# Norm factors spread over the partitions by a row in DRAM, and a new TensorE order for the first stage, in a hybrid decoder layer

## The chip, the core and the metric

The kernel runs on one core of a Trainium2 chip. Its time is the device time of one execution in microseconds (us); lower is better. The core has five engines that run side by side: TensorE (PE in the profile: matrix products into PSUM; PEld is its weight loading), VectorE (DVE), ScalarE (ACT), GpSimd (POOL) and SyncE (SP), which here issues nearly all DMAs. Each engine works its own list of instructions strictly in order, and an instruction that waits holds up everything behind it on its engine. That holds for SP's list of DMAs too.

## The reference

2048 prompt tokens and 8 decode tokens (2056 columns in the kernel) pass one layer of width 1024:

```python
xn = rmsnorm(x, norm1_g)
xr, gr, q, k, v = split(xn @ w_in)                  # 512 | 512 | 512 | 128 | 128
rec = rglru(causal_conv(xr)) * gelu(gr)             # gated recurrence over the tokens
att = sink_attention(q, k, v)                       # window of 128 earlier tokens, 8 heads on 2 kv heads
h = x + concat(rmsnorm(rec), rmsnorm(att)) @ w_out
hn = rmsnorm(h, norm2_g)
y = h + (silu(hn @ w_gate) * (hn @ w_up)) @ w_down  # 2816 wide
out = rmsnorm(y, final_norm_g)
# rmsnorm(x, g) = x * rsqrt(mean(x*x) + 1e-6) * g
```

There are five norms (x, rec, att, h, y). Each gives one factor per token. Activations lie with the features on the 128 partitions and the tokens along the free dimension, so a factor has to be present on all partitions as a row over the tokens before DVE can multiply with it.

## The kernel before

**Tiling.** The first part takes the tokens in four pieces (SUBS: 520 columns, then three of 512). For piece s the names end in s: input projection (ip, 14 column blocks of w_in, each by three products of high and low parts), conv, gates (g) and scan, attention items (s, pt, o), the norms of the two groups (rc for the recurrence, at for attention), output projection (op) and the norm of h. The second part is the FFN in three token groups (gi 0, 1, 2), each in two halves of 342 or 344 columns (HALVES), over 11 pairs of column blocks of w_gate, w_up and w_down. A pair is computed by seven products of sums of blocks (Strassen's scheme) for gate (ps_g), up (ps_u) and down (pd or pw); the sums of weight blocks are made by ACT, DVE and POOL out of loaded pieces (ru, rg, rd) or loaded ready-made (w_u from split_u, w_g from split_g). DVE adds the products up in SBUF: c_g, c_u for gate and up, y for down. A PSUM tile such as ps_g 1 is taken by two of the seven products in turn, so the second can start only when DVE has added up the first. finish applies the last norm to a group that is done while TensorE is already in the next group (gi 0 and 1); finish_last does it for gi 2 at the end.

**A norm factor before the change.** The sums of squares (acc) go through TensorE against a column of constants (st_...), which leaves a factor's argument per token in columns: cols[p, j] belongs to token j*w + p of the piece (w is 104, 128, 86 or 114; j up to 5). DVE adds epsilon, POOL raises to the power -1/2. row_bcast then makes the row: for each j one fp32 product of the column, repeated along the free dimension as stationary operand, with the identity, into a PSUM tile (bc_...), which ACT copies to SBUF (rb_...). Products are padded by filler products (w_...) where a table asks for it. half_bcast does the same for the norm of h out of the tile rs2, once for each half (hb).

**What sets the order.** Steps are generators (yield t) that run by planned time; the time becomes a priority, and a scheduler places the instructions of every engine by it, with one exception: TensorE's list from the start to the second pair of group 0 is written out by hand in the table PE_ORDER (name of a step, a colon, number of its products). All engines but TensorE, and TensorE behind the table, follow the scheduler. Buffers rotate: rb tiles have 3, hb tiles 2, ready-made weights (wp, wp2) 5 and 3, the PSUM tile of st, bc, hb and g has 1. A DMA on SP waits also until the eighth before it has landed.

Of the kernel before, what the change touches and what calls it, by code (L numbers as in the profile page):

```python
# [112 lines left out]
w_st_x0:13 ip0_1_0 ip0_1_1 w_st_x0:4 ip0_12_0 ip0_12_1 ip0_1_0:2 ip0_1_1:2 ip0_12_0:2 ip0_12_1:2 ip0_1_0 ip0_1_1  # L113
ip0_12_0 ip0_12_1 ip0_1_0:2 ip0_1_1:2 ip0_12_0:2 ip0_12_1:2 ip0_1_0 ip0_1_1 ip0_12_0 ip0_12_1 ip0_1_0:2 ip0_1_1:2
ip0_12_0 ip0_1_0 ip0_1_1 ip0_12_0:2 ip0_12_1:3 ip0_1_0:2 ip0_1_1 ip0_1_0 ip0_1_1:2 ip0_12_0:3 ip0_12_1:3 ip0_1_0:3
ip0_1_1:3 ip0_12_0 ip0_1_0:2 ip0_1_1:2 ip0_12_0 ip0_1_0 ip0_1_1 ip0_12_0:4 ip0_12_1:6 ip0_1_0:3 ip0_1_1:3 ip0_12_0:3
ip0_1_0:2 ip0_1_1:2 ip0_12_0:2 ip0_12_1:5 ip0_9_0:5 st_x0:5 ip0_9_0:9 ip0_9_1:24 ip0_9_0:10 bc_x0_0:4 ip0_8_0:24
ip0_8_1:4 bc_x0_4 ip0_8_1:20 ip0_0_0:24 ip0_0_1:23 g0_1_0_0 ip0_0_1 ip0_3_0:24 g0_1_0_260 ip0_3_1:17 g0_1_1_0
ip0_3_1:7 ip0_11_0:18 g0_1_1_260 ip0_11_0:6 ip0_11_1:15 vt0_0 ip0_11_1:9 ip0_10_0:23 vt0_1 ip0_10_0 ip0_10_1:24
ip0_13_0:10 vt0_2 ip0_13_0:14 ip0_13_1:6 vt0_3 ip0_13_1:18 ip0_2_0:7 s0_0_0:4 ip0_2_0:5 g0_0_0_0 s0_0_1:4 ip0_2_0:12  # L120
ip0_2_1:6 s0_1_0:4 s0_1_1:4 ip0_2_1:2 g0_0_0_260 ip0_2_1:13 pt0_0_1:4 ip0_2_1 s1_0_0:4 ip0_2_1:2 ip0_5_0:3 s1_0_1:4
ip0_5_0 g0_0_1_0 ip0_5_0:9 o0_0_0 ip0_5_0:11 ip0_5_1 s1_1_0:4 ip0_5_1:2 pt0_1_1:4 o0_0_0 ip0_5_1:4 g0_0_1_260
ip0_5_1:12 s1_1_1:2 o0_1_0 s1_1_1:2 ip0_5_1:5 ip0_4_0:6 s2_0_0:4 ip0_4_0:3 o0_1_0 ip0_4_0:11 pt1_0_0:4 ip0_4_0:2
s2_0_1:4 ip0_4_0:2 ip0_4_1:24 ip1_8_0:15 ip0_6_0:2 o1_0_0 ip0_6_0:8 pt1_0_1 o1_0_0 pt1_0_1:3 ip0_6_0 ip1_8_0
g0_3_0_0 ip0_6_0:13 ip0_6_1 ip1_8_0:2 ip0_6_1:15 o1_0_1 g0_3_0_260 s2_1_0:4 ip0_6_1 ip1_8_0 ip0_6_1 pt1_1_0
ip0_6_1:5 o1_0_1 s2_1_1:4 pt1_1_0:3 ip0_6_1 ip1_8_0:5 ip1_9_0 g0_3_1_0 ip1_9_0:19 ip0_7_0:9 ip1_9_0:2 pt1_1_1 o1_1_0
pt1_1_1:3 g0_3_1_260 ip1_9_0:2 ip0_7_0:2 o1_1_0 ip0_7_0:13 w_bc_x1_0 bc_x1_0 s3_0_0:3 s3_0_1:4 ip0_7_1 s3_0_0
ip0_7_1 o1_1_1:2 bc_x1_0 w_pt2_0_0:4 ip0_7_1 bc_x1_0 ip0_7_1 bc_x1_0 ip0_7_1:2 pt2_0_0:4 ip0_7_1:18 ip1_10_0:2
o2_0_0:2 pt2_0_1:3 g0_2_0_0 ip1_10_0:12 pt2_0_1 ip1_10_0:10 ip1_11_0:2 o2_0_1 ip1_11_0 s3_1_0:4 pt2_1_0:4 g0_2_0_260
ip1_11_0 s3_1_1:4 ip1_11_0:2 o2_0_1 ip1_11_0:11 g0_2_1_0 pt2_1_1:3 ip1_11_0:7 ip1_4_0:4 o2_1_0 ip1_4_0 pt2_1_1  # L130
ip1_4_0 o2_1_0 g0_2_1_260 ip1_4_0:18 ip1_0_0:2 o2_1_1 ip1_0_0 vt1_0 ip1_0_0:6 dS:2 o2_1_1 pt3_0_0:4 ip1_0_0:5 dS:6
ip1_0_0:6 o3_0_0 ip1_0_0:4 ip1_12_0:2 dS2:2 ip1_12_0:2 pt3_0_1 o3_0_0 ip1_12_0:2 pt3_0_1:3 ip1_12_0:18 ip1_13_0:6
o3_0_1 ip1_13_0:2 o3_0_1 ip1_13_0:3 pt3_1_0:4 ip1_13_0:9 dS3 ip1_13_0 dS3 ip1_13_0:3 ip1_1_0:8 pt3_1_1:2 o3_1_0
pt3_1_1 ip1_1_0:2 pt3_1_1 o3_1_0 dS4:4 s4_0_0 ip1_1_0:2 o3_1_1 s4_0_1:3 s4_0_0:3 s4_0_1 dS4:4 ip1_1_0 o3_1_1
ip1_1_0:11 ip1_5_0:6 dS5:2 s4_1_0:2 s4_1_1:4 ip1_5_0 vt1_1 ip1_5_0:3 s4_1_0:2 ip1_5_0:8 pt4_0_0:2 ip1_5_0 pt4_0_0:2
ip1_5_0:5 ip1_2_0:2 s5_0_0:4 ip1_2_0 s5_0_1:4 ip1_2_0 vt1_2 ip1_2_0:8 o4_0_0 ip1_2_0:6 pt4_0_1 o4_0_0 pt4_0_1:3
ip1_2_0:3 vt1_3 ip1_2_0:3 o4_0_1 s5_1_0:4 s5_1_1:4 o4_0_1 st_rc0 pt4_1_0:4 st_rc0:4 ip1_6_0:15 pt4_1_1:4 bc_rc0_0:3
# [1592 lines left out]
```

## Time and profile before

| | us |
|---|---|
| median of 3 runs (2059.78, 2065.76, 2065.12) | 2065.12 |
| span of the profiled execution, first to last instruction | 2054.6 |
| TensorE busy (98% of the span) | 2015.9 |
| VectorE busy (71%) | 1459.9 |
| ScalarE busy (46%) | 944.6 |
| GpSimd busy (44%) | 906.5 |

The profiled execution's own time is its span, 2054.6, and what lies around it before the first and after the last instruction, which the profile does not show; the median of the runs is 10.5 above the span. A row of a group reads: line, engine, operation, output<-inputs with tile numbers left out, count | busy us, mean ns of one | idle time of the engine just before, with what ended it. A row of the timeline reads: start, us, engine, line, operation, count, and in brackets idle time and its releaser. A matrix product in fp32 leaves two records. On average TensorE runs at a granted clock of 0.997 of full speed.

### The profile page before, as it was taken

The numbers are of one execution on the slowest core, as the hardware profiler recorded it, in microseconds if no ns is written. First come the engines' busy times: TensorE is split into PE (matmuls) and PEld (weight loads), VectorE is DVE, ScalarE is ACT, GpSimd is POOL, SyncE is SP. The second block draws the span as 40 slices with busy tenths as digits, with TensorE's granted clock in tenths as the row PEclk, the third lists the DMA queues.
The fourth block names the chain that finished last, engine by engine and source line by source line (L and its number), as shares of the span: only waits on it lengthen the run. The fifth ranks groups of instructions, "written<-read, shape, count | busy, mean of one in ns | idle before, by whom it ended". The sixth has DMA issues, their size and how long they took to land.

```text
span 2054.6 us, 34857 instructions
## 1 busy us (share of the span) xinstructions
PE 2015.9 (98%) x12319; PEld 1908.1 (93%) x12319; DVE 1459.9 (71%) x2694; ACT 944.6 (46%) x1960; POOL 906.5 (44%) x799
## 2 busy tenths in 40 slices
PE   9999999999999999999999999999999999999998
PEld 9988787878777899999999999999999999999998
DVE  6877886767985766666654667777768666777675
ACT  6764774553664543343334533333335433433343
POOL 5311342020122787567656645556457522322333
PEclk9999999999999999999999999999999999999999
DMA  9864584576688856666546677776677675566652
GB/s 329 293 213 143 188 275 159 175 233 210 208 261 280 314 200 223 205 210 207 207 172 210 229 260 258 227 229 221 222 253 265 211 251 189 183 197 196 197 179 96
DMA packets 208991, 450.98 MB, mean 219 GB/s; under 512 B 25232, under 2 KB 82720, under 8 KB 208800
## 3 DMA queue, kind: packets, MB, share of 16 engines
q1 hardware_dynamic: 205184, 445.73, 65.2%
q10 hardware_dynamic: 3632, 3.02, 0.4%
q8 instruction: 97, 1.59, 0.3%
q14 instruction: 78, 0.64, 0.1%
HBM read 335.89 MB, written 113.84 MB: 219 GB/s over the span
## 4 chain that ended last, share of the span: by engine, by line
PE 77%; DVE 9%; DMA 6%; ACT 3%; issue 2%; POOL 1%; SPq 0%; DVEq 0%; ACTq 0%; POOLq 0%
PE ps_u L396 19%; PE ps_g L396 19%; PE pw L396 11%; PE pd L396 10%; PE ip L396 10%; PE op L396 4%; DMA n<-hs 3%; DMA xs<-in_xT 1%; DMA m<-mixed 1%; PE o L396 1%; PE pt L401 1%; DVE sc L974 1%; DVE sc L963 1%; PE s L396 1%; DMA mixed<-n 1%
## 5 line engine op out<-in xcount | busy, mean ns | idle before, releaser
L396 PE MATMUL ps_g<-hn,w_g 128*128 128x342 f32 (+1 forms) x2772 | 489.4, 320 | 4.6 <-DVE c_u L1410 1.8
L396 PE MATMUL ps_u<-hn,w_u 128*128 128x342 f32 (+1 forms) x2772 | 479.9, 319 | 1.9 <-ACT c_u L1436 1.3
L396 PEld LDWEIGHTS ps_g<-hn,w_g 128*128 128x128 f32 x2772 | 445.1, 188 | 6.0 <-DVE c_u L1410 2.3
L396 PEld LDWEIGHTS ps_u<-hn,w_u 128*128 128x128 f32 x2772 | 444.2, 188 | 2.6 <-ACT c_u L1436 1.6
L396 PE MATMUL ip<-xn,w_in 128*128 128x512 f32 (+1 forms) x1680 | 353.4, 358 | 1.9 <-ACT xn L431 1.8
L396 PEld LDWEIGHTS ip<-xn,w_in 128*128 128x128 f32 x1680 | 270.1, 189 | 46.0 <-issue 3.8
L1500 DVE TENSOR_TENSOR y<-y,pw 128x342 f32<-128x342 f32 x504 | 238.7, 504 | 73.0 <-PE pw L396 72.2
L396 PE MATMUL pd<-fh,w_d 128*128 128x344 f32 (+1 forms) x960 | 239.4, 320 | 0.6 <-DVE y L1469 0.6
L396 PE MATMUL op<-mix,w_out 128*128 128x512 f32 (+1 forms) x960 | 203.4, 357 | 0.5 <-DVE rrec L763 0.3
L396 PEld LDWEIGHTS op<-mix,w_out 128*128 128x128 f32 x960 | 155.4, 188 | 29.3 <-issue 5.0
L1469 DVE TENSOR_TENSOR y<-y,pd 128x344 f32<-128x344 f32 (+1 forms) x240 | 117.9, 507 | 75.3 <-PE pd L396 70.7
L396 PEld LDWEIGHTS pd<-fh,w_d 128*128 128x128 f32 x960 | 168.3, 188 | 1.4 <-DVE y L1469 1.1
L396 PE MATMUL pw<-fh,wd 128*128 128x342 f32 x576 | 165.6, 319 | 1.2 <-DVE y L1500 1.2
L396 PE MATMUL pd<-fl,w_d 128*128 128x344 f32 (+1 forms) x480 | 153.4, 320 | 0.0
L1381 DVE TENSOR_TENSOR fl<-c_u,fh 128x342 fp32r<-128x342 f32 (+1 forms) x132 | 107.1, 815 | 48.3 <-ACT fh L1380 47.9
L1225 POOL TENSOR_TENSOR w_u<-ru,w_u 128x512 fp32r<-128x512 f32 x44 | 58.9, 1338 | 181.6 <-ACT w_u L1224 155.0
L1392 POOL TENSOR_TENSOR c_u<-c_u,c_g 128x342 f32<-128x342 f32 (+1 forms) x60 | 60.5, 1008 | 170.7 <-DVE c_u L1410 132.1
L1380 ACT CAST fh<-c_u 128x342 fp32r<-128x342 f32 (+1 forms) x132 | 63.0, 480 | 157.8 <-POOL c_u L1392 61.9
L396 PE MATMUL pw<-t,wd 128*128 128x342 f32 x648 | 126.7, 320 | 2.6 <-DVE t L1381 1.7
L1410 DVE TENSOR_TENSOR c_u<-c_u,ps_u 128x342 f32<-128x342 f32 (+1 forms) x99 | 50.2, 507 | 100.3 <-PE ps_u L396 100.1
L396 PEld LDWEIGHTS pw<-t,wd 128*128 128x128 f32 x648 | 106.0, 188 | 4.4 <-DVE t L1381 2.5
L396 PEld LDWEIGHTS pw<-fh,wd 128*128 128x128 f32 x576 | 105.3, 189 | 1.7 <-DVE y L1500 1.5
(316 smaller groups left out, 3507.4 us busy)
## 6 DMA issues: line engine op xcount, KB each, us to landing
w_g<-split_g SPq DMA_DIRECT2D x88, 512.0 KB, 4.2
w_u<-split_u SPq DMA_DIRECT2D x88, 512.0 KB, 4.9
w_in<-split_w SPq DMA_DIRECT2D x84, 512.0 KB, 3.5
rg<-in_wgate SPq DMA_DIRECT2D x110, 256.0 KB, 3.1
ru<-in_wup SPq DMA_DIRECT2D x110, 256.0 KB, 3.2
w_out<-split_w SPq DMA_DIRECT2D x48, 512.0 KB, 4.4
split_g<-w_g SPq DMA_DIRECT2D x44, 512.0 KB, 3.6
split_u<-w_u SPq DMA_DIRECT2D x44, 512.0 KB, 2.7
```

What stands on the lines that cost most here:

```text
L396: r = nc.tensor.matmul(*args, **kw)
L401: r = nc.tensor.transpose(*args)
L963: seen[f"sm{gb}_{kv}_{g}"] = nc.vector.tensor_tensor_reduce(sc[:, g, :kn], ps[:, gi * 256:gi * 256 + kn], mask[:, k0:k0 + kn], -SCALE, ns[ ...
L974: nc.vector.tensor_scalar(sc[:, g, :kn], sc[:, g, :kn], mx[:, 1, g:g + 1], None, ALU.mult)
L1225: lo_eng.tensor_tensor(w[:, 1, :], src, w[:, 0, :].bitcast(F32), op=ALU.subtract)
L1380: nc.scalar.copy(hi, v)
L1381: nc.vector.tensor_tensor(lo, v, hi.bitcast(F32), ALU.subtract)
L1392: (nc.vector if p == NPAIR - 1 or src is not v else eng(E_MUL[2 * h + n])).tensor_tensor(v, src, g, op=ALU.mult)
L1410: nc.vector.tensor_tensor(o, a, b, op)
L1469: r = nc.vector.tensor_tensor(ys[gi, n, m], ys[gi, n, m], ps, ALU.add)
L1500: nc.vector.tensor_tensor(v, v, ps, ALU.add)
```

## The change

1. A DRAM tile hrow holds the factors of h as one row for all tokens. row_store writes columns to a row in DRAM by a DMA (element by element, in token order); row_fetch stores to a row of its own and loads that row back to all 128 partitions by a second DMA, which waits on SP for the first to land.
2. The norms of x for pieces 1 to 3, of rec for pieces 0 to 2, and of y for groups 0 and 1 (both halves) use row_fetch. x of piece 0, rec of piece 3, all of at, and finish_last keep row_bcast.
3. The norm of h is stored to hrow when each piece's factors are ready (4 stores), and half_bcast is one load from it (6 in all).
4. The table PE_ORDER is written anew, without the removed products. For example the run `w_st_x0:13 ip0_1_0 ip0_1_1 w_st_x0:4` becomes `w_st_x0:17 ip0_1_0 ip0_1_1`, and `ip0_9_0:5 st_x0:5 ip0_9_0:9 ip0_9_1:24` becomes `ip0_9_0:14 ip0_9_1:15 st_x0:5 ip0_9_1:9`.

```diff
+        hrow = dp.tile([1, NTOK], F32, name="hrow")
...
+        def row_store(cols, w, nt, name, row):
+            nc.sync.dma_start(row.rearrange("o (j p) -> (o p) j", p=w), cols)
+
+        def row_fetch(cols, w, nt, name):
+            row = dp.tile([1, w * nt], F32, name=f"row_{name}")
+            row_store(cols, w, nt, name, row)
+            out = bcp.tile([P, TM], F32, tag="bc", name=f"rb_{name}")
+            nc.sync.dma_start(out[:, :w * nt], row.to_broadcast([P, w * nt]))
+            return out
...
         def half_bcast(gi, n, name):
             o, nn = HALVES[gi][n]
             out = hbp.tile([P, TP], F32, tag="hb", name=f"hb_{name}")
-            ps = m_tile(f"hb_{name}")
-            for s, (c0, T, _, w, nt) in enumerate(SUBS):
...
-                        mm(f"hb_{name}", ps[:, x - o:y - o], rs2[:w, s, j:j + 1].to_broadcast([w, P]),
-                                         ident[:w, d0:d0 + y - x], start=True, stop=True)
-            nc.scalar.copy(out[:, :nn], ps[:, :nn])
+            nc.sync.dma_start(out[:, :nn], hrow[:, o:o + nn].to_broadcast([P, nn]))
             return out
...
-                state[s]["bc"] = row_bcast(cols[:w, :nt], w, nt, f"x{s}")
+                state[s]["bc"] = (row_fetch if s else row_bcast)(cols[:w, :nt], w, nt, f"x{s}")
...
-                bc = row_bcast(cols[:w, :nt], w, nt, f"{name}{s}")
+                bc = (row_fetch if name == "rc" and s < 3 else row_bcast)(cols[:w, :nt], w, nt, f"{name}{s}")
...
                     rstd_cols(acc[:, :T], w, nt, 0, rs2[:w, s, :nt], f"h{s}")
+                    row_store(rs2[:w, s, :nt], w, nt, f"h{s}", hrow[:, c0:c0 + T])
...
-                bc = row_bcast(cols[:w, :nt], w, nt, name, 0, False, True)
+                bc = row_fetch(cols[:w, :nt], w, nt, name)
...
                 rstd_cols(acc[:, :T], w, nt, 0, rs2[:w, s, :nt], f"h{s}", 0, True)
+                row_store(rs2[:w, s, :nt], w, nt, f"h{s}", hrow[:, c0:c0 + T])
```

**TensorE at the recurrence norm of piece 0** (about 200 us into the span). In the names, xc is the convolved branch, s and pt are attention products, ip_6_0 is block 6 of the input projection of piece 1, g_0_0_0 and g_0_1_0 are the two gate products of the first channel block, st_at<-ones are the fillers ahead of the attention norm's sums. Before:

```order
L401 MATMUL pt_1_1_2358<-cs,sc_1_2323 128x128 x4
L396 MATMUL bc_rc_0_2217<-cs,rccols_2207 128x104 x3
L396 MATMUL s_0_0_2467<-KK,qst_0_2414 128x256
...
L396 MATMUL bc_rc_4_2223<-cs,rccols_2207 128x104
L401 MATMUL pt_0_0_2396<-cs,sc_0_2370 128x128 x3
L396 MATMUL g_0_0_0_2665<-xc_0_2201,gw 128x512
L396 MATMUL g_0_1_0_2668<-xc_0_2201,gw 128x512
L396 MATMUL st_at_2793<-ones 128x256 x13
```

And after:

```order
L397 MATMUL g_0_0_0_2656<-xc_0_2198,gw 128x512
L397 MATMUL s_0_1_2465<-KK,qst_0_2405 128x256
L397 MATMUL s_0_1_2465<-KL,qst_0_2405 128x256
L397 MATMUL g_0_1_0_2659<-xc_0_2198,gw 128x512
L402 MATMUL pt_0_0_2387<-cs,sc_0_2361 128x128 x4
L397 MATMUL s_0_1_2465<-KK,qst_0_2405 128x256
L397 MATMUL ip_6_0_2850<-xn_3_1464,w_in_6_0_2745 128x512 x3
L397 MATMUL ip_6_0_2850<-xn_4_1469,w_in_6_1_2747 128x512 x3
L397 MATMUL st_at_2784<-ones 128x256
L397 MATMUL ip_6_0_2850<-xn_5_1474,w_in_6_1_2747 128x512 x3
```

The bc_rc products are gone, two attention products stand between the two gate products, and products of ip_6_0 that stood ahead of the gates now stand between them and the fillers.

**DVE at the finish of group 0** (about 1185 us). The y rows with rb_f are the scalings by the final norm; c_g_1_11 takes the PSUM tile ps_g_1_1 of the next group's first pairs. Before:

```order
L453 TENSOR_SCALAR cols_f_0_13143<-st_f_0_13144 86x4
L1410 TENSOR_TENSOR c_g_1_11_7353<-c_g_1_11_7353,ps_g_1_1_13126 128x342
L1520 SCALAR_TENSOR_TENSOR y_0_8158<-y_0_8158,vec,rb_f_1_13214 128x344
L1520 SCALAR_TENSOR_TENSOR y_1_8167<-y_1_8167,vec,rb_f_1_13214 128x344
...
L1520 SCALAR_TENSOR_TENSOR y_2_8185<-y_2_8185,vec,rb_f_1_13214 128x344
L1469 TENSOR_TENSOR y_0_13187<-y_0_13187,pd_0_0_0_13325 128x342
```

And after:

```order
L454 TENSOR_SCALAR cols_f_0_13098<-st_f_0_13099 86x4
L1520 SCALAR_TENSOR_TENSOR y_0_8121<-y_0_8121,vec,rb_f_1_13171 128x344
L1520 SCALAR_TENSOR_TENSOR y_1_8130<-y_1_8130,vec,rb_f_1_13171 128x344
...
L1520 SCALAR_TENSOR_TENSOR y_2_8148<-y_2_8148,vec,rb_f_1_13171 128x344
L1469 TENSOR_TENSOR y_0_13142<-y_0_13142,pd_0_0_0_13274 128x342
L1410 TENSOR_TENSOR c_g_1_11_7325<-c_g_1_11_7325,ps_g_1_1_13081 128x342
```

The addition c_g_1_11 stood ahead of the eight scalings and now stands behind them and one addition to y.

**SP at the same place.** out_yT stores a finished row of the output, y<-hs loads h for the next group's sums, w_u_1_5 and w_u_1_7 are ready-made weights of the next group's pair 1. Before:

```order
L1521 DMA out_yT<-y_2_8185 128x344
L1343 DMA sums_d<-sd_1_13615 128x512
L1248 DMA w_u_1_5_13431<-split_u 128x1024
L1220 DMA y_2_13237<-hs 128x342 x2
L1521 DMA out_yT<-y_0_8158 128x344
```

And after:

```order
L1521 DMA out_yT<-y_2_8148 128x344
L481 DMA rb_f_0_13194<-row_f_0_13192 128x344
L1220 DMA y_2_13189<-hs 128x342 x3
L1248 DMA w_u_1_6_13362<-split_u 128x1024
L1236 DMA rg_2_01_13466<-in_wgate 128x512
...
L1220 DMA y_4_13250<-hs 128x342 x3
L1220 DMA y_5_13267<-hs 128x342
L1248 DMA w_u_1_5_13380<-split_u 128x1024
L1248 DMA w_u_1_7_13400<-split_u 128x1024
```

The load w_u_1_5 stood between the two sets of eight out_yT and now stands behind the fetch rb_f_0, the second set and all loads of y.

More of the change, by code (lines that the diff above doesn't have):

```diff
@@ L112 @@
 PE_ORDER = """
[L113 to L137, printed above, removed]
@@ new lines @@
+ip0_12_0 ip0_1_0:2 ip0_1_1:2 ip0_12_0 ip0_1_0 ip0_1_1 ip0_12_0:4 ip0_12_1:6 ip0_1_0:3 ip0_1_1:3 ip0_12_0:3 ip0_1_0:2
+ip0_1_1:2 ip0_12_0:2 ip0_12_1:5 ip0_9_0:14 ip0_9_1:15 st_x0:5 ip0_9_1:9 ip0_9_0:10 bc_x0_0:4 ip0_8_0:24 ip0_8_1:4
+bc_x0_4 ip0_8_1:20 ip0_0_0:24 ip0_0_1:23 g0_1_0_0 ip0_0_1 ip0_3_0:24 g0_1_0_260 ip0_3_1:17 g0_1_1_0 ip0_3_1:7
+ip0_11_0:18 g0_1_1_260 ip0_11_0:6 ip0_11_1:15 vt0_0 ip0_11_1:9 ip0_10_0:23 vt0_1 ip0_10_0 ip0_10_1:24 ip0_13_0:10
+vt0_2 ip0_13_0:14 ip0_13_1:6 vt0_3 ip0_13_1:18 ip0_2_0:7 s0_0_0:4 ip0_2_0:5 g0_0_0_0 s0_0_1:4 ip0_2_0:12 ip0_2_1:6
@@ new lines @@
+o1_0_1 s2_1_1 pt1_1_0:3 ip0_6_1 ip1_8_0:5 ip1_9_0 g0_3_1_0 ip1_9_0:19 ip0_7_0:9 ip1_9_0:2 pt1_1_1 o1_1_0 pt1_1_1:3
+g0_3_1_260 ip1_9_0:2 ip0_7_0:2 o1_1_0 ip0_7_0:13 s3_0_0:3 s3_0_1:4 ip0_7_1 s3_0_0 ip0_7_1 o1_1_1:2 w_pt2_0_0:4
+ip0_7_1:4 pt2_0_0:4 ip0_7_1:18 ip1_10_0:13 o2_0_0:2 pt2_0_1:3 g0_2_0_0 ip1_10_0 pt2_0_1 ip1_10_0:10 ip1_11_0:2 o2_0_1
+ip1_11_0 s3_1_0:4 pt2_1_0:4 g0_2_0_260 ip1_11_0 s3_1_1:4 ip1_11_0:2 o2_0_1 ip1_11_0:11 g0_2_1_0 pt2_1_1:3 ip1_4_0
+ip1_11_0:7 ip1_4_0:3 o2_1_0 ip1_4_0 pt2_1_1 ip1_4_0 o2_1_0 g0_2_1_260 ip1_4_0:18 ip1_0_0:2 o2_1_1 ip1_0_0 vt1_0
@@ new lines @@
+ip1_0_0:6 dS pt3_0_0:2 dS o2_1_1 pt3_0_0:2 ip1_0_0:4 dS ip1_0_0 dS ip1_0_0 dS:4 ip1_0_0:5 o3_0_0 ip1_0_0:4 ip1_12_0:2
+dS2:2 pt3_0_1 o3_0_0 ip1_12_0:2 pt3_0_1:3 ip1_12_0:18 ip1_13_0:6 o3_0_1 ip1_13_0:2 o3_0_1 ip1_13_0 ip1_12_0:2
+ip1_13_0:2 pt3_1_0:4 ip1_13_0:9 dS3:2 ip1_1_0:5 ip1_13_0 ip1_1_0:6 ip1_13_0:3 ip1_1_0:4 pt3_1_1:2 o3_1_0 pt3_1_1
+ip1_1_0:2 pt3_1_1 o3_1_0 dS4:2 s4_0_0:3 dS4 s4_0_0 ip1_1_0:2 o3_1_1 s4_0_1:4 dS4 ip1_5_0 dS4:4 ip1_1_0 o3_1_1
+ip1_1_0:4 ip1_5_0:6 dS5:2 s4_1_0:2 s4_1_1:4 vt1_1 ip1_5_0:3 s4_1_0:2 ip1_5_0:8 pt4_0_0:2 ip1_5_0 pt4_0_0:2 ip1_5_0:5
@@ new lines @@
+vt3_0 ip3_11_0:5 ip3_13_0:3 pt11_0_1 o11_0_0:2 ip3_13_0 pt11_0_1:3 ip3_13_0:4 vt3_1 ip3_13_0:16 o11_0_1 ip3_0_0:3
+o11_0_1 vt3_2 ip3_0_0:5 pt11_1_0:4 ip3_0_0:16 s12_0_0:4 ip3_4_0 s12_0_1 o11_1_0 s12_0_1:2 pt11_1_1 o11_1_0 pt11_1_1
+vt3_3 pt11_1_1:2 s12_0_1 ip3_4_0:16 s12_1_0:4 ip3_4_0:5 o11_1_1 s12_1_1:4 ip3_4_0:2 ip3_1_0:2 g3_0_0_0 ip3_1_0:2
+s13_0_0 pt12_0_0 o11_1_1 pt12_0_0 ip3_1_0 pt12_0_0:2 ip3_1_0:5 ip3_6_0:3 s13_0_0:3 ip3_1_0:7 s13_0_1:4 ip3_1_0:4
+g3_0_1_0 ip3_1_0:3 ip3_6_0:13 o12_0_0 ip3_6_0:8 ip3_5_0:4 pt12_0_1 ip3_5_0 pt12_0_1:2 ip3_5_0 o12_0_0 st_at2:4
@@ new lines @@
+pt13_1_1:3 o13_1_0 pt13_1_1 op2_2_0:4 op2_3_0:12 g3_3_0_0 op2_3_0:4 o13_1_1 op2_3_0 s15_0_0 pt14_0_0:4 s15_0_1:2
+o13_1_1 s15_0_0:3 s15_0_1:2 g3_3_1_0 op2_3_0:7 op2_4_0:12 o14_0_0 op2_4_0:2 pt14_0_1 o14_0_0 pt14_0_1:3 op2_4_0:10
+op2_5_0:12 s15_1_0:2 op2_5_0 s15_1_0 s15_1_1:2 o14_0_1 s15_1_1:2 s15_1_0 op2_5_0:5 o14_0_1 op2_5_0:6 op2_6_0
+pt14_1_0:4 op2_6_0:23 op2_7_0 o14_1_0 op2_7_0:2 pt14_1_1:3 op2_7_0:2 pt14_1_1 op2_7_0:5 o14_1_0 op2_7_0:2 o14_1_1
+op2_7_0:7 st_rc3:2 w_pt15_0_0:2 o14_1_1 op2_7_0 st_rc3:2 pt15_0_0:4 w_bc_rc3_0 op2_7_0:4 bc_rc3_0:4 o15_0_0 pt15_0_1
@@ new lines @@
+g0_0_6:12 u0_0_1:12 g0_0_7:12 g0_0_3:12 g0_0_4 w_ps_u0_0_2:4 u0_0_2:7 g0_0_4:5 u0_0_2:2 g0_0_4 u0_0_2 u0_0_6:12
+u0_0_2:2 g0_0_4:5 u0_0_5:12 u0_0_7:12 g0_1_1:12 u0_0_4:12 u0_0_3:12 g0_1_6:12 g0_1_2:12 g0_1_5:12 d0_0_0_0:6
+d0_0_0_1:6 d0_0_1_0:3 g0_1_7:12 d0_0_1_0:3 g0_1_3:12 d0_0_1_1:6 d0_0_2_0:3 g0_1_4:12 d0_0_2_0:3 d0_0_3_0:6 d0_0_2_1:6
+d0_0_3_1:6 d0_0_4_0:6 d0_0_4_1:6 u0_1_1:2 d0_0_5_0:6 d0_0_5_1:6 d0_0_6_0:6 u0_1_1 d0_0_6_1:6 d0_0_7_0:6 d0_0_7_1:6
+u0_1_1:9 u0_1_2:12 u0_1_5:12 u0_1_6:12 u0_1_7:12 u0_1_4:12 u0_1_3:12
@@ L481, in half_bcast @@
             out = hbp.tile([P, TP], F32, tag="hb", name=f"hb_{name}")
-            ps = m_tile(f"hb_{name}")
-            for s, (c0, T, _, w, nt) in enumerate(SUBS):
-                a, b = max(o, c0), min(o + nn, c0 + T)
-                if a >= b:
-                    continue
-                j0, j1 = (a - c0) // w, (b - c0 - 1) // w + 1
-                with ahead():
-                    for j in range(j0, j1):
-                        x, y = max(a, c0 + j * w), min(b, c0 + j * w + w)
-                        d0 = x - c0 - j * w
-                        mm(f"hb_{name}", ps[:, x - o:y - o], rs2[:w, s, j:j + 1].to_broadcast([w, P]),
-                                         ident[:w, d0:d0 + y - x], start=True, stop=True)
-            nc.scalar.copy(out[:, :nn], ps[:, :nn])
+            nc.sync.dma_start(out[:, :nn], hrow[:, o:o + nn].to_broadcast([P, nn]))
             return out
```

101 lines of the change are left out of this document (48 added, 53 removed).

## The prediction

> **What bounds the kernel now.** I read the page's first part, the chain that ended last, the groups of TensorE, and then the stretches of the timeline where the change lands.
>
> ```profile
> PE 2015.9 (98%) x12319; PEld 1908.1 (93%) x12319; DVE 1459.9 (71%) x2694; ACT 944.6 (46%) x1960; POOL 906.5 (44%) x799
> PE 77%; DVE 9%; DMA 6%; ACT 3%; issue 2%; POOL 1%; SPq 0%; DVEq 0%; ACTq 0%; POOLq 0%
> ```
>
> TensorE is busy for 2015.9 of 2054.6 us, so only 38.7 us of the span are idle on it, and no other engine is above 71%. A product taken off TensorE therefore shortens the run by its own length, unless TensorE then waits for what replaces it. Both sides of that sentence have to be priced: the products removed, and the waits that the DMAs put in their place.
>
> **What is removed.** These are the groups of TensorE (busy us, mean ns of one):
>
> ```profile
> L396 PE MATMUL hb<-cs,rs 128*128 128x128 f32 (+11 forms) x44 | 5.6, 268 | 0.0
> L396 PE MATMUL bc_f<-cs,cols_f 114*128 114x114 f32 (+1 forms) x40 | 5.4, 274 | 0.1
> L396 PE MATMUL bc_x<-cs,xcols 128*128 128x128 f32 (+1 forms) x34 | 5.3, 273 | 0.0
> L396 PE MATMUL bc_rc<-cs,rccols 128*128 128x128 f32 (+1 forms) x34 | 4.8, 276 | 0.7 <-POOL rccols L454 0.7
> ```
>
> Each product leaves two records. Gone are all 44 of hb, 28 of the 40 of bc_f (the last group keeps 12), 24 of the 34 of bc_x (x0 keeps 10) and 26 of the 34 of bc_rc (rc3 keeps 8): 122 records, 61 products. By busy time that is 5.6 + 5.4 x 28/40 + 5.3 x 24/34 + 4.8 x 26/34 = 16.8 us. Busy time of one counts its drain, though, so I price a product by the distance between starts:
>
> ```profile
> 1183.22 0.63 PE L396 MATMUL ps_g<-hn,w_g 128*128 128x342 f32 x3
> 1183.69 1.02 PE L396 MATMUL bc_f<-cs,cols_f 86*128 86x86 f32 x8
> 1184.50 0.72 PE L396 MATMUL ps_g<-hn,w_g 128*128 128x342 f32 x3
> 1185.06 0.33 PE L396 MATMUL pd<-fh,w_d 128*128 128x342 f32 x1
> ```
>
> Eight records (four products) hold TensorE from 1183.69 to 1184.50, 0.81 us. The three ps_g after them take 0.56 to the next start against 0.47 for the three ahead, so the switch costs another 0.09: 0.90/4 = 0.225 us a product. 61 x 0.225 = **13.7 us**, which I take; the ends are 61 x 0.2025 = 12.4 without the switch, and 16.8 by busy time. The copies that ACT made out of PSUM go as well (46% busy, worth nothing). In their place stand 30 DMAs on SP's queue: 14 stores of a row and 16 fetches.
>
> **What a store and a fetch cost.** No row of before has either shape, so I bound them by the nearest ones. The last number is us from issue to landing.
>
> ```profile
> mixed<-n SPq DMA_DIRECT2D x56, 171.0 KB, 2.5
> n<-hs SPq DMA_DIRECT2D x32, 171.0 KB, 3.7
> m<-mixed SPq DMA_DIRECT2D x28, 172.0 KB, 4.6
> out_sh_o<-q ACTq DMA_DIRECT2D x4, 4.0 KB, 2.1
> out_pconv<-hist ACTq DMA_DIRECT2D x1, 6.0 KB, 2.0
> out_phs<-carry ACTq DMA_DIRECT2D x1, 2.0 KB, 5.2
> ```
>
> A store moves 1.3 to 2.1 KB out of SBUF: 2.0 to 5.2 us, and I take the mean of the three small rows, 3.1. A fetch fills 128 partitions with 1.4 or 2 KB each: 2.5 to 4.6, and I take 3.7, the load of the same size from DRAM. The fetch waits on SP for the store to land, so store and fetch make 6.8 us in series (4.5 to 9.8), where the products and the ACT copy took under 2. Everything depends on who waits for those 6.8 us.
>
> A rule of the Trainium skill gives less. Its page "DMA: Bandwidth & Descriptors", section "Anatomy of one DMA", gives a DMA as about 2.0 us fixed plus its bytes at 436 GB/s, by which my estimate is 2.0 for the store and 2.4 for the fetch, 4.4 together. The sum would then lose both finish terms below and be -15.0, 2050.1; the trace puts the load n<-hs at 3.7, so I keep the rows.
>
> **Finish of groups 0 and 1.** Here DVE used to run the 8 scalings of y after c_g; now they stand ahead of the c_g addition that empties the PSUM tile ps_g which the products of w_g_1_4 fill next. In each row below: start, length, then the instruction.
>
> ```profile
> 1178.57 1.29 POOL L454 TENSOR_TENSOR cols_f<-cols_f,nhalf 86x4 f32<-86x4 f32 x1
> 1628.64 1.13 POOL L454 TENSOR_TENSOR cols_f<-cols_f,nhalf 114x3 f32<-114x3 f32 x1
> 1180.94 0.33 SPq L1343 DMA_DIRECT2D sums_d<-rd  x1
> 1185.76 4.32 DVE L1520 SCALAR_TENSOR_TENSOR y<-y,vec,rb_f 128x344 f32<-128x344 f32 x8
> 1635.73 3.98 DVE L1520 SCALAR_TENSOR_TENSOR y<-y,vec,rb_f 128x342 f32<-128x342 f32 x8 [0.18 <-ACT rb_f L470]
> 1190.00 0.50 DVE L1469 TENSOR_TENSOR y<-y,pd 128x342 f32<-128x342 f32 x1
> 1190.42 0.68 DVE L1225 TENSOR_TENSOR w_u<-ru,w_u 128x512 fp32r<-128x512 f32 x1
> 1180.46 3.39 PE L396 MATMUL ps_g<-hn,w_g 128*128 128x342 f32 x20
> 1196.01 3.75 PE L396 MATMUL ps_u<-hn,w_u 128*128 128x342 f32 x23
> 1199.60 0.32 PE L396 MATMUL pd<-fh,w_d 128*128 128x342 f32 x1
> 1631.18 2.28 PE L396 MATMUL ps_g<-hn,w_g 128*128 128x342 f32 x13
> ```
>
> A product of 342 columns takes (1199.60 - 1196.01)/23 = 0.156 us. In group 0 the new order has 63 of them between the end of st_f_0 (1180.46) and the first of w_g_1_4, so TensorE is there at 1180.46 + 63 x 0.156 = 1190.3. The factors are ready on POOL at 1179.86; two issues of 0.33, store, fetch, 4.32 of scalings, then one y and one c_g addition of 0.50 end at 1185.8 + (store + fetch). So TensorE waits as soon as store and fetch exceed 4.5: by 6.8 it waits **2.3 us**, between 0 and 5.3. In group 1 there are 66 products from 1631.18, so 1641.5; DVE is done at 1629.77 + 0.66 + 3.98 + 0.50 + 0.68 + 0.50 = 1636.1 + (store + fetch): at 1642.9, **1.4 us** of wait, between 0 and 4.4.
>
> The second thing late there is a weight. SP issues in order, and w_u_1_5 now stands behind both sets of 8 out_yT and seven loads of y.
>
> ```profile
> 1648.93 3.39 SPq L1220 DMA_DIRECT2D y<-hs  x7
> w_u<-split_u SPq DMA_DIRECT2D x88, 512.0 KB, 4.9
> ```
>
> Its landing in group 0 is 1179.86 + 2 x (0.33 + 4.32 + 0.33) + 0.33 for the third issue + 3.39 + 4.9 = 1198.4, plus one store and two fetches (10.5) = 1208.9. TensorE comes to it after 169 products, 1180.46 + 26.4 = 1206.8, plus the 2.3 already waited, 1209.1: no further wait, by a hair. In group 1, where two more loads of y (0.97) stand ahead, the same sum gives 1659.1 against 1631.18 + 181 x 0.156 = 1659.4.
>
> **First stages.** At rc0 the four scalings of rrec now wait on DVE for the fetch:
>
> ```profile
> 199.25 1.18 POOL L454 TENSOR_TENSOR rccols<-rccols,nhalf 104x5 f32<-104x5 f32 x1 [1.89 <-DVE rccols L453]
> 207.13 2.77 DVE L866 SCALAR_TENSOR_TENSOR rrec<-rrec,vec,rb_rc 128x520 f32<-128x520 f32 x4
> 597.00 1.28 DVE L521 SCALAR_TENSOR_TENSOR n<-n,vec,hb 128x344 f32<-128x344 f32 x2 [3.79 <-DMA n<-hs]
> 604.04 1.78 PE L396 MATMUL op<-mix,w_out 128*128 128x512 f32 x7
> w_out<-split_w SPq DMA_DIRECT2D x48, 512.0 KB, 4.4
> ```
>
> The row is there at 200.43 + 0.66 + 6.8 = 207.9 (205.6 to 210.9), against 207.13 before, and the reciprocal and the scalings of sc for item 5 now queue behind it. What hides this is ip6, ip3 and ip7 on TensorE; if that cover is short, pt5 is late next. I take 0.5, between 0 and 3. The fetches for x1, x2, x3, rc1, rc2 and the halves of h stand on SP far ahead of their readers; I cost them at nothing. The closest is hb_1_0: it waits for a buffer which DVE last reads at 597.00 to 597.64, and holds up w_out_6_0 behind it, which then lands at 597.6 + 0.66 + 4.4 = 602.7, ahead of the op run at 604.04 in which TensorE takes it.
>
> The order of TensorE's first stage is set anew around these idle times (in brackets, with what ended them):
>
> ```profile
> 21.11 1.08 PE L396 MATMUL st_x<-avg,xacc 128*104 128x1 f32 x10 [0.77 <-DVE xacc L443]
> 206.57 1.12 PE L396 MATMUL g<-xc,gw 128*128 128x512 f32 x2 [0.21 <-ACT rb_rc L470]
> 208.48 1.13 PE L396 MATMUL g<-xc,gw 128*128 128x512 f32 x2 [0.78 <-ACT ra L802]
> 211.33 3.09 PE L396 MATMUL st_at<-ones 128*128 128x256 f32 x13 [1.73 <-ACT ia L802]
> ```
>
> 24 products of ip0_9 now stand ahead of st_x0, and products of ip1_6 between the gates and the run of st_at. They can fill up to 0.77 + 0.21 + 0.78 + 1.73 = 3.5 us; moved work can open other gaps, so I take half, **1.8**, between 0 and 3.5.
>
> **The sum.** -13.7 - 1.8 + 2.3 + 1.4 + 0.5 = **-11.3 us** against the profiled execution. Its span is 2054.6; the median of the three runs, 2065.12, stands 10.5 above it, which I take as unchanged (launch and end lie around the span, and the runs spread from 2059.78 to 2065.76). So 2065.1 - 11.3 = **2053.8**. The ends: -16.8 - 3.5 = -20.3 (2044.8), and -12.4 + 5.3 + 4.4 + 3 = +0.3 (2065.4).
>
> **Rivals.**
>
> *It is given back at the finishes.* The first 3.1 of the store may be wrong: the row's elements lie 86 or 114 apart, so the store may go out as 344 pieces of 4 bytes. The row of the queue with the smallest packets says what a piece costs:
>
> ```profile
> q10 hardware_dynamic: 3632, 3.02, 0.4%
> ```
>
> 0.4% of 16 engines' 2054.6 us over 3632 packets is 36 ns. Spread over 16 engines, 344 pieces take 0.8 us, on one 12.4. Halfway, 6.6 with the 2.0 of the shortest row, makes the store 8.6 in group 0 and its wait 7.8 instead of 2.3; the total is -5.8, and with the long fetch of 4.6 at both finishes (1.8 more) and nothing recovered (1.8) it is -2.2: 2059 to 2063, no change that can be told (0.3% is 6.2 us, about the least that a measurement of this kernel tells from nothing). For it: no wait of TensorE in before has such a DMA in it, so the term is unmeasured. Against: out_sh_o landed in 2.1.
>
> The Trainium skill has this rule, in the same page: a last dimension that is not contiguous becomes one descriptor per element ("Rules for kernel authors"), and a DMA runs on the largest number of engines up to 16 that divides the slowest dimension ("Why a DMA increments its semaphore by 16"). For 86 partitions that is two engines; by my estimate 172 x 36 ns = 6.2 us, a store of 8.2 and a total of -6.2. No run here shows it yet.
>
> *More is gained.* DMAs land at the short ends (2.0 and 2.5), no finish waits, the idle times close: -13.7 - 3.5 = -17.2, 2047.9, and 2044.8 with the busy price. The skill's 2.0 us fixed would be this case.
>
> *Slower.* One mechanism: SP's queue is blocked at each finish by a store, then two fetches in a row, so w_u_1_5 is late. The wait is (store + 2 fetches) - 8.4 us in group 0 and - 10.8 in group 1. It cancels 13.7 + 1.8 and adds 6.2 once 2 x (store + 2 fetches) - 19.2 passes 21.7, that is at 20.5, or 6.8 us a DMA: from there it is above 2071. 5.2 is the longest row of a small store, 4.6 that of a load this size, so I see little for it.
>
> **Chances.** The forecast's case, -6.2 to -16, 0.58 (2049 to 2058.9); given back 0.22; more gained 0.12; slower 0.08. So faster 0.70, within 0.3% 0.22, slower 0.08. The range, 2046 to 2065, leaves out the slower case and the ends of the sum.
>
> **What the next profile would show.** Groups: hb gone, bc_f x12, bc_x x10, bc_rc x8; TensorE busy 13 to 17 us less. DMA issues: row and rb rows, with landings near 3.1 and 3.7. Waits: ps_g behind DVE c_g at about 1180 and 1630 less the gain so far, of 0 to 5 us; ps_u behind a DMA there would be the slower rival. Around 200 us the idle ahead of st_at should be under 1.73. I am wrong if the stores take over 7 us, if DVE's wait at rc0 reaches TensorE through pt5, or if the new order opens gaps of its own between 60 and 300 us.

## The result

The changed kernel takes 2144.38 us (median of 4 runs, 2142.69 to 2146.17) against 2062.45 for the kernel before beside it: a ratio of 1.0402, 95% interval 1.0383 to 1.0420. It is 82 us slower, where 11 us less were forecast. First the page's lines that answer to those of before (span, busy time of each engine, the chain that ended last):

```profile
span 2140.9 us, 34641 instructions
PE 2036.4 (95%) x12196; PEld 1919.4 (90%) x12196; DVE 1459.5 (68%) x2694; ACT 937.3 (44%) x1943; POOL 910.5 (43%) x799
PE 65%; DMA 14%; DVE 12%; ACT 3%; issue 3%; POOL 2%; SPq 1%; DVEq 0%; ACTq 0%; POOLq 0%
```

The span is 86.3 us longer (the 82 us above compare medians; the profiled execution of before was one of its faster ones). TensorE is idle for 2140.9 - 2036.4 = 104.5 us, 65.8 more than before. Its busy time grew too, by 20.5 us, though the products are gone (12196 records for 12319); with it, the mean granted clock fell from 0.997 to 0.976. DMAs hold 14% of the chain for 6%. Next the largest waits of TensorE, two of DVE, and those of SP's queue for a store (us in total, times, longest):

```profile
PE pd L397 <- DVE y L1469: 14.6, 3, 7.4
PE o L397 <- DVE ratt L996: 14.2, 3, 10.8
PE o L397 <- ACT pth L983: 12.9, 4, 8.9
PE ps_g L397 <- DVE c_g L1410: 10.2, 2, 5.8
...
DVE y L1520 <- DMA rb_f<-row_f: 36.7, 4, 10.4
DVE rrec L865 <- DMA rb_rc<-row_rc: 33.6, 3, 14.2
...
SPq L481 <- DMA row_rc<-rccols: 23.5, 3, 10.5
SPq L493 <- DMA hrow<-rs: 22.3, 3, 7.7
SPq L481 <- DMA row_f<-cols_f: 12.2, 2, 6.6
```

None of these waits of TensorE is for a DMA; it waits for DVE and ACT, and DVE for rows that SP has not fetched. SP itself stood still for up to 10.5 us at a time behind one store of 1.3 to 2 KB. Where the time went is read from one instruction that both kernels have, POOL's power for a norm, in the timeline of after:

```profile
201.56 1.18 POOL L455 TENSOR_TENSOR rccols<-rccols,nhalf 104x5 f32<-104x5 f32 x1 [1.17 <-DVE rccols L454]
484.08 1.02 POOL L455 TENSOR_TENSOR rccols<-rccols,nhalf 128x4 f32<-128x4 f32 x1 [12.93 <-DVE rccols L454]
680.24 1.02 POOL L455 TENSOR_TENSOR rs<-rs,nhalf 128x4 f32<-128x4 f32 x1 [6.49 <-DVE rs L454]
1236.92 1.29 POOL L455 TENSOR_TENSOR cols_f<-cols_f,nhalf 86x4 f32<-86x4 f32 x1
1699.83 1.13 POOL L455 TENSOR_TENSOR cols_f<-cols_f,nhalf 114x3 f32<-114x3 f32 x1
```

and of before, as far as the prediction does not show them:

```profile
457.06 1.14 POOL L454 TENSOR_TENSOR rccols<-rccols,nhalf 128x4 f32<-128x4 f32 x1 [5.93 <-DVE rccols L453]
632.46 1.02 POOL L454 TENSOR_TENSOR rs<-rs,nhalf 128x4 f32<-128x4 f32 x1 [7.57 <-DVE rs L453]
```

The delay is 2.3 us at rc0, 27.0 at rc2, 47.8 at the norm of h for piece 2, 58.4 at the finish of group 0, 71.2 at that of group 1, and 86.3 at the end. The delay follows the stores more than the length of a stretch: 47.8 us come with the eight stores of the first 680 us, 10.6 in the next 557 with two, and 12.8 and 15.1 with the two at each finish.

One such place in full, rc1, on SP, DVE and TensorE:

```profile
317.97 0.32 SPq L475 DMA_DIRECT2D hrow<-rs  x1
318.39 0.38 SPq L381 DMA_DIRECT2D w_in<-split_w  x1
326.06 0.32 SPq L493 DMA_DIRECT2D hb<-hrow  x1
326.48 0.39 SPq L475 DMA_DIRECT2D row_rc<-rccols  x1
326.95 0.46 SPq L381 DMA_DIRECT2D w_in<-split_w  x1
334.78 0.32 SPq L481 DMA_DIRECT2D rb_rc<-row_rc  x1
...
339.79 2.74 DVE L865 SCALAR_TENSOR_TENSOR rrec<-rrec,vec,rb_rc 128x512 f32<-128x512 f32 x4 [14.20 <-DMA rb_rc<-row_rc]
...
341.86 0.79 PE L397 MATMUL o<-pth,vt 128*128 128x512 f32 x1 [8.88 <-ACT pth L983]
```

SP stores hrow and then has nothing to do but wait for it, 318.39 to 326.06, since the next DMA reads it. Behind that stands the store of rc1, whose factors POOL had done at 321.87; the fetch of its row waits in turn from 326.95 to 334.78. DVE stands still for 14.20 us, the attention work behind it is late, and TensorE is idle for 8.88. Two stores in a row take about 8 us each, where the forecast had given 3.1.

The stores do more than land late. Around the store of x1, which nobody waits for before the fetch 12 us later, the windows of before and after read (columns: busy us of TensorE, its weight loads, DVE, ACT and POOL with counts, granted clock, DMA share, GB/s; of before first):

```profile
50.00:56.00 6.00, 6.00 (x52) 5.97 (x51) 4.14 (x10) 4.00 (x8) 4.16 (x3) 1.00 0.95 323
56.00:63.00 7.00, 7.00 (x61) 7.00 (x60) 4.12 (x8) 2.39 (x6) 4.18 (x4) 1.00 0.99 340
63.00:70.00 7.00, 7.00 (x60) 6.94 (x59) 5.35 (x15) 5.00 (x12) 2.17 (x3) 1.00 0.99 351
...
50.00:56.00 6.00, 6.00 (x53) 6.00 (x52) 4.73 (x10) 3.73 (x8) 3.67 (x3) 1.00 0.92 302
56.00:63.00 7.00, 6.85 (x58) 6.64 (x56) 3.00 (x6) 0.89 (x2) 1.85 (x2) 1.00 1.14 97
63.00:70.00 7.00, 3.88 (x20) 3.89 (x21) 2.84 (x5) 4.16 (x9) 2.61 (x3) 0.76 1.02 323
```

From 56 to 63 us the whole core moves 97 GB/s in place of 340, while its DMA engines read as fully busy. So one store of 2 KB goes with a hold-up of the core's transfers as a whole. TensorE pays a little later: in the 7 us after, it is busy for 3.88 and its granted clock is down to 0.76.

### The profile page after: what moved, and what is told of

It reads as the page before. It is cut to its first block, busy times and chain, and to the rows that moved or that the text cites. A ratio compares the mean times of both kernels' runs of the same rounds, so it can differ in the third digit from the quotient of the medians.

```text
span 2140.9 us, 34641 instructions
## 1 busy us (share of the span) xinstructions
PE 2036.4 (95%) x12196; PEld 1919.4 (90%) x12196; DVE 1459.5 (68%) x2694; ACT 937.3 (44%) x1943; POOL 910.5 (43%) x799
## 3 DMA queue, kind: packets, MB, share of 16 engines
q1 hardware_dynamic: 214166, 449.09, 65.8%
## 4 chain that ended last, share of the span: by engine, by line
PE 65%; DMA 14%; DVE 12%; ACT 3%; issue 3%; POOL 2%; SPq 1%; DVEq 0%; ACTq 0%; POOLq 0%
PE ps_u L397 18%; PE ps_g L397 17%; PE pw L397 10%; PE pd L397 10%; PE ip L397 7%; DMA n<-hs 3%; DMA m<-mixed 1%; DMA row_rc<-rccols 1%; DMA raw_in<-in_win 1%; PE op L397 1%; DVE sc L973 1%; DMA hrow<-rs 1%; DVE n L520 1%; DMA hs<-xres 1%; DMA rb_rc<-row_rc 1%
## 5 line engine op out<-in xcount | busy, mean ns | idle before, releaser
L397 PE MATMUL ps_g<-hn,w_g 128*128 128x342 f32 (+1 forms) x2772 | 494.9, 322 | 14.4 <-DVE c_g L1410 10.2
L397 PEld LDWEIGHTS ps_g<-hn,w_g 128*128 128x128 f32 x2772 | 450.7, 191 | 17.1 <-DVE c_g L1410 10.8
L397 PE MATMUL ip<-xn,w_in 128*128 128x512 f32 (+1 forms) x1680 | 361.1, 362 | 2.5 <-DMA w_in<-split_w 0.9
L397 PEld LDWEIGHTS ip<-xn,w_in 128*128 128x128 f32 x1680 | 275.0, 193 | 48.3 <-issue 3.8
L397 PE MATMUL pd<-fh,w_d 128*128 128x344 f32 (+1 forms) x960 | 244.2, 327 | 14.9 <-DVE y L1469 14.6
L397 PE MATMUL op<-mix,w_out 128*128 128x512 f32 (+1 forms) x960 | 210.3, 365 | 5.0 <-DVE xres L1129 4.2
L397 PEld LDWEIGHTS pd<-fh,w_d 128*128 128x128 f32 x960 | 173.7, 194 | 16.4 <-DVE y L1469 15.7
L1224 ACT CAST w_u<-ru 128x512 fp32r<-128x512 f32 x99 | 61.5, 621 | 130.8 <-PE pd L397 52.4
```

Source lines behind the costliest of these rows:

```text
L397: r = nc.tensor.matmul(*args, **kw)
L1224: nc.scalar.copy(w[:, 0, :], src)
```

## Experiments

**Three theories for the first four runs.** A: a store in 4-byte pieces holds up all DMAs of the core for some us, by the number of its pieces. B: any store and fetch in series on SP cost this. C: the new TensorE order opens the gaps.

*Larger pieces, nothing else.*

```diff
-            nc.sync.dma_start(row.rearrange("o (j p) -> (o p) j", p=w), cols)
+            nc.sync.dma_start(row.rearrange("o (p j) -> (o p) j", p=w), cols)
```

> The changed kernel, but each store writes the row partition by partition, so in pieces of 12 to 20 bytes in place of 4 (128 pieces in place of 512); the factors land in another token order, which leaves the numbers of the output wrong and all instructions and waits alike. Theory A (a store in 4-byte pieces holds up every DMA of the core for some 6 us, in proportion to its pieces): stores land in 3 to 5 us, time 2055 to 2085. Theory B (any store and fetch in series on SP's queue costs this, pieces or not): stores land in 5 us or more, time 2115 to 2145. Theory C (the new TensorE order opens the gaps): 2135 to 2150.

Measured 2062.91 against 2062.99 for before: ratio 1.0009, 0.9996 to 1.0022. The store of rc0 and the fetch that waits for it, in after and then in this run:

```profile
202.76 0.33 SPq L475 DMA_DIRECT2D row_rc<-rccols  x1
208.91 0.34 SPq L481 DMA_DIRECT2D rb_rc<-row_rc  x1
...
197.91 0.34 SPq L475 DMA_DIRECT2D row_rc<-rccols  x1
199.28 0.34 SPq L481 DMA_DIRECT2D rb_rc<-row_rc  x1
```

6.15 us became 1.37. All 82 us hang on how the row is cut into pieces; B and C are out as main causes. A's landing of 3 to 5 us was too pessimistic here. One reservation: in groups 1 and 2 (behind about 1650 us) the scheduler also set some work of TensorE, DVE and SP in another order than in the changed kernel. The runs below with one piece and with spread pieces keep TensorE's order in full and come out lower still.

*Stores as they are, but nobody waits for them.*

```diff
+        zrow = dp.tile([1, 17 * P], F32, name="zrow")   # filled once with ones
...
-            nc.sync.dma_start(out[:, :w * nt], row.to_broadcast([P, w * nt]))
+            nc.sync.dma_start(out[:, :w * nt], zrow[:, :w * nt].to_broadcast([P, w * nt]))
```

> The changed kernel with all 14 stores as they are, but every fetch reads a constant row that was written once at the start, so no fetch waits for a store (the factors are left out of the result). Theory A: the stores still hold up all other DMAs, time 2075 to 2125. Theory B: the series is gone, time 2048 to 2060. Theory C: 2120 to 2145.

Measured 2129.49, ratio 1.0329 (1.0292 to 1.0367), a little above A's range and inside C's, so this run alone doesn't tell A from C. Much of the loss is there with nobody waiting for a store; the next run shows how much of it is the stores'.

*No store either.*

```diff
-            nc.sync.dma_start(row.rearrange("o (j p) -> (o p) j", p=w), cols)
+            pass
```

> As the run with the constant row, but with no store at all (16 fetches of the constant row are left, the factors are left out of the result). Theories A and B: 2045 to 2058, the products saved and nothing given back. Theory C: 2120 to 2145.

Measured 2086.12, ratio 1.0119 (1.0062 to 1.0176), which no theory had. A fetch that depends on nothing was placed elsewhere by the scheduler (the first hb is DMA 26 of SP's list in place of 209), and the other engines' lists were made anew around it. With these lists the kernel is 23 us slower than before without any store. But the rearrangement is the same in both runs of the constant row: TensorE's and POOL's orders are alike in them, and SP's, without the stores, differs in seven DMAs by a few places. So the 43.4 us between the two runs are, but for that, the price of 14 stores that nobody waits for: 3.1 us each.

*The order of before on TensorE*, less the removed entries (a table, not shown).

> The changed kernel with the TensorE order of the kernel before, less the entries of the removed products. Theories A and B: within 12 us of the changed kernel, 2132 to 2156. Theory C: 2055 to 2075.

Measured 2139.55, ratio 1.0378 (1.0335 to 1.0421). C is out; this interval overlaps with that of the changed kernel, so which order is the better one here can't be told.

**Is it the number of pieces, or that they are neighbours?** Theory A split in two. In these two runs the order on TensorE is that of the changed kernel, and so, but for one or two swaps of neighbours, is the order on SP.

*One piece per store:*

```diff
-            nc.sync.dma_start(row.rearrange("o (j p) -> (o p) j", p=w), cols)
+            nc.sync.dma_start(row[:, :nt], cols[0:1, :])
```

> The changed kernel, but each store writes one piece of 12 to 20 bytes (the first partition's factors) into a row that was filled at the start from x, so all waits and the order on SP stay and only the pieces go from 512 to 1 (the factors are left out of the result). If what the run with 16-byte pieces still gave back against the 13.7 us saved was left over from its 128 pieces: 2050 to 2057. If it is the wait for the fetch and what stands behind it (theory D): 2060 to 2067, within 4 us of the run with 16-byte pieces.

Measured 2057.17 against 2060.99: ratio 0.9977 (0.9967 to 0.9988). It sits at the border of the two expectations: faster than with 128 pieces by 0.3%, and a gain of 3.8 us where 11 were forecast.

*As many 4-byte pieces, 512 bytes apart:*

```diff
-            nc.sync.dma_start(row.rearrange("o (j p) -> (o p) j", p=w), cols)
+            nc.sync.dma_start(row[:, :w * nt * P].rearrange("o (j p e) -> (o p) j e", p=w, e=P)[:, :, 0], cols)
```

> The changed kernel with its 4-byte pieces, as many as before, but each written 512 bytes behind the last one in DRAM; the fetches read the first part of that region, most of which was filled at the start (the factors are left out of the result). Theory A1 (it is neighbouring 4-byte writes, which fall into the same line of DRAM and are worked off one after another): 2055 to 2080. Theory A2 (it is the number of pieces): 2130 to 2155.

Measured 2057.81: ratio 0.9977 (0.9963 to 0.9990), the same as with one piece. The number of pieces costs nothing that shows. A1 holds as far as it says that neighbouring pieces are what costs; what becomes of them in DRAM no run shows.

**The stores alone, in the kernel before.** This is the cleanest measure: no product removed, TensorE's list as it was, 14 stores added into rows that nobody reads.

```diff
+                if s:
+                    spare(cols[:w, :nt], w, nt, f"x{s}")    # row_store to a row of its own
                 state[s]["bc"] = row_bcast(cols[:w, :nt], w, nt, f"x{s}")
...
```

> The kernel before, with its products and its TensorE order, and 14 stores in 4-byte pieces added at the places where the changed kernel has them, into rows that nobody reads. Theory A: each store holds up the loads for some us, time 2090 to 2130. Theories B and C: 2062 to 2070, 14 issues on SP and nothing else.

Measured 2107.14 against 2060.99: ratio 1.0218 (1.0197 to 1.0238), 46 us or 3.3 us a store. Its windows at the same place:

```profile
56.00:63.00 7.00, 7.00 (x61) 7.00 (x59) 3.34 (x6) 0.89 (x2) 1.84 (x2) 1.00 1.20 102
63.00:70.00 7.00, 4.03 (x24) 3.83 (x22) 2.76 (x5) 4.08 (x9) 2.56 (x2) 0.80 0.96 327
```

102 GB/s, close to the 97 of the changed kernel. So 46 of the 82 us, a little over half, need no wait for a store; the rest is likely the waits for the stores to land, which were not measured apart. Then the same stores with their pieces 64 and 512 bytes apart. The orders on SP, DVE, POOL and TensorE are in both runs exactly those of the run that took 2107.14:

```diff
-            nc.sync.dma_start(row.rearrange("o (j p) -> (o p) j", p=w), cols)
+            nc.sync.dma_start(row.rearrange("o (j p e) -> (o p) j e", p=w, e=16)[:, :, 0], cols)   # e=128 for 512 bytes
```

> The kernel before with 14 unread stores in 4-byte pieces, as in the run that took 2107, but with the pieces 64 bytes apart in DRAM in place of 4. If the hold-up comes from several pieces in one stretch of up to 64 bytes: 2060 to 2070. If the stretch is longer (some hundred bytes): 2075 to 2107.

Measured 2061.82, ratio 1.0008 (0.9998 to 1.0018).

> The kernel before with the same 14 unread stores, pieces 512 bytes apart. Theory A1 (neighbouring pieces): 2060 to 2068, as many pieces as in the run that took 2107 and no cost but the issues. If the number of pieces had a share in those 46 us: 2075 to 2107.

Measured 2061.80, ratio 1.0007 (0.9992 to 1.0021). At 64 bytes the whole effect is gone:

```profile
56.00:63.00 7.00, 7.00 (x61) 7.00 (x60) 4.07 (x8) 2.29 (x5) 4.72 (x4) 1.00 1.02 360
```

360 GB/s, where the pieces 4 bytes apart left 102. That settles it: the same elements, the same lists, and only the distance in DRAM differs. Steps between 4 and 64 bytes were not run.

**A version for use?** The columns can be cut so that a partition holds neighbouring tokens; then its piece of 12 to 20 bytes is in token order and the result is whole. The store is that of the first run above, and the tokens of x are loaded in the same cut.

```diff
+            a3 = acc[:, :w * nt].rearrange("q (p j) -> q p j", j=nt)
...
-                    r = mm(f"st_{name}", ps[:w, j:j + 1], acc[:, j * w:(j + 1) * w], avg[:, which:which + 1],
+                    r = mm(f"st_{name}", ps[:w, j:j + 1], a3[:, :, j] if by else acc[:, j * w:(j + 1) * w], avg[:, which:which + 1],
...
```

At all places:

> The changed kernel computing the full result with rows in 16-byte pieces: the sums of squares are taken over every third to fifth token, so that a partition holds neighbouring tokens and its piece of the row is in token order. The order on SP and TensorE is the changed kernel's. Theory A: as the run with 16-byte pieces and wrong token order, 2058 to 2068. If the strided sums cost TensorE or the order matters more than that: 2068 to 2080.

Measured 2067.96 against 2060.79: ratio 1.0040 (1.0025 to 1.0055), where the two expectations meet. The strided sums do cost TensorE. The products of the sums for h, before and here:

```profile
L396 PE MATMUL st_h<-avg,hacc 128*128 128x1 f32 (+1 forms) x34 | 3.9, 232 | 0.0
L397 PE MATMUL st_h<-avg,hacc 128*128 128x1 f32 (+1 forms) x34 | 7.1, 315 | 0.0
```

With those for rec (4.0 to 6.6) and for the last norm (4.4 to 6.1) TensorE is busy 7.5 us more. The orders on TensorE, SP, DVE and POOL are those of the run with 16-byte pieces and wrong token order (with the reservation made there), and the ratio is 0.3% above that run's, some 6 us: the strided sums are what the right token order costs.

With the last norm by products again:

> As the version with rows in 16-byte pieces in token order at all places, but the last norm of groups 0 and 1 by products as in the kernel before (14 products back, 3.1 us). Theory D (with cheap stores the loss sits at the finishes, where DVE stands behind two fetches and w_u_1_5 behind them): 2050 to 2058, below both the kernel before and the version with all places. If the finishes cost no more than their products: 2062 to 2068.

Measured 2062.10: ratio 1.0007 (0.9993 to 1.0020). It lies in the range for finishes that cost no more than their products, and theory D's range was missed. Yet bringing 14 products back made it 5.9 us faster than with rows at all places, 1.7 of them from the sums of the last norm, which are not strided here. So the finishes do cost more than they save, but the kernel is no faster than before. TensorE's waits at the finish of group 1, in the version with rows at all places:

```profile
1647.64 2.16 PE L397 MATMUL ps_g<-hn,w_g 128*128 128x342 f32 x12 [0.78 <-DVE c_g L1411]
1659.22 0.43 PE L397 MATMUL pd<-fh,w_d 128*128 128x342 f32 x1 [4.55 <-DVE y L1470]
```

Both waits are gone with the products back. Rows for x and h alone, with the TensorE order of before:

> A version for use: the sums of squares are taken over every fourth (fifth) token, so that a partition holds neighbouring tokens and a store in 16-byte pieces is in token order; rows in DRAM for x1 to x3 and h alone, products with the identity for rec and the last norm as in the kernel before, the TensorE order of before less the removed entries. 34 products fewer, 7.6 us. Theory D (the loss that is left lies at rec and the finishes, where DVE stands behind the fetch): 2053 to 2060 against about 2063. If instead the stores still hold up loads or the halves of h come late: 2060 to 2070.

Measured 2065.46 against 2060.99: ratio 1.0018 (1.0007 to 1.0029). Theory D's range was missed here too. 34 products fewer, and not faster: of the 7.6 us, 3.4 go to the strided sums for h (3.9 to 7.3 us busy), and where the rest goes was not traced. No version tried with its full result beats the kernel before.

## Why the prediction was wrong

**The step that failed** is "What a store and a fetch cost": a store was given 3.1 us, between 2.0 and 5.2, from three small stores of before, and nothing else was charged for it. Its landing was 6.15 us at rc0, and SP stood for up to 10.5 us behind one. Worse, the step took a DMA's price to be its own latency. The price here is what it does to all others, 3.3 us of the kernel for each store with no one waiting, and that term had no place in the sum. The three rows were near in bytes but not in pattern: they write 16 to 48 bytes from each partition, the store 4 at a time. How the bytes lie in DRAM was the thing to match. The prediction named stores of over 7 us as a sign that it is wrong, and most came to that.

**The rival of the pieces** named the right suspect and the wrong mechanism. It charged 344 pieces by packet time on few engines; as many pieces spread out cost nothing. By my estimate from the Trainium skill's rules ("DMA: Bandwidth & Descriptors", "Rules for kernel authors" and "Why a DMA increments its semaphore by 16 and not by 1"), group 0's store would be 8.2 us. Its fetch started 7.14 us after it (1238.24 to 1245.38), but that nearness is luck. The chosen k does not explain the loss: stores from 128 partitions, which run on 16 engines by that rule, were as slow: 8.30 us at rc1, where the same sum gives an estimate of 2.0 + 512 x 0.036 / 16 = 3.2. The skill's 2.0 us fixed (same page, "Anatomy of one DMA") is given there for DMAs that GpSimd issues, which the prediction did not say. SP's store in larger pieces took 1.37 us, less than that, and the one in 4-byte pieces 6.15.

**The slower rival** had half of the form that came true (SP blocked and its rows late, though not the weight that it named) and the point, 6.8 us a DMA, which most of the stores did pass; but I placed it at the finishes alone, gave it 0.08, and left the first stages at 0.5 us. 47.8 of 86.3 us were lost before the norm of h for piece 2. The words "far ahead of their readers; I cost them at nothing" were wrong for rc1, where DVE waited 14.20 us behind two stores in series, and for rc2, where it waited 13.06 us behind one.

**The finishes.** 2.3 us was forecast for the wait behind c_g in group 0 and 1.4 in group 1; with slow stores it was 5.79 and 4.45. Group 0's, and the wait that came after it:

```profile
1255.44 3.79 PE L397 MATMUL ps_g<-hn,w_g 128*128 128x342 f32 x12 [5.79 <-DVE c_g L1410]
1268.51 0.65 PE L397 MATMUL pd<-fh,w_d 128*128 128x342 f32 x1 [3.17 <-DVE y L1469]
```

The second row shows a wait that the forecast lacked: the additions of y stand behind the second set of scalings on DVE, and the products pd wait for them. Even with 16-byte pieces in token order this was 4.55 us in group 1, where the wait behind c_g was down to 0.78. So it was this, and not w_u_1_5, that was late next.

**The products** were removed as counted (bc_f 12, bc_x 10, bc_rc 8 records left):

```profile
L397 PE MATMUL bc_f<-cs,cols_f 114*128 114x114 f32 x12 | 1.7, 281 | 0.1
L397 PE MATMUL bc_rc<-cs,rccols 128*128 128x128 f32 x8 | 1.6, 372 | 0.0
L397 PE MATMUL bc_x<-cs,xcols 104*128 104x104 f32 x10 | 1.4, 270 | 0.0
```

What they are worth is shown only in sum: with stores of one piece the kernel gained 3.8 us (2057.17 against 2060.99), about a third of the forecast's 11.3. Most of the missing 7.5 us lies in waits. In that run's profile TensorE is idle for 2055.9 - 2008.8 = 47.1 us, 8.4 more than before, where the forecast's waits less its recovered idle time make 2.3 + 1.4 + 0.5 - 1.8 = 2.4 more. That is an estimate from one profile of each kernel. Of the 47.1 us, 4.3 are pd behind the additions of y; how the rest splits between the waits for fetches in the first stages and the new lists was not separated.

**The order:** 1.8 us of recovered idle time could not be seen beside the rest; with the old order the time was 2139.55 against 2144.38.

**The base:** the 10.5 us between span and median were launch and end only in small part: in the changed kernel an execution's time is 1.8 us above its span (2142.69 against 2140.9). This moved the level of the forecast, not its sum.

## What to carry to other kernels

Before a column is written to DRAM element by element, look at how the elements lie: neighbouring 4-byte pieces held up the core's DMAs as a whole here, and the same pieces 64 bytes apart did not. A transfer's price is not only its latency: compare GB/s of the whole core just after its issue with a stretch without it. And where a fetch waits for a store on an in-order queue, count what stands behind it there, the next store included.
